# First transfers of memory and weights together, keys in another order, and mLSTM values side by side, in a decoder block on one core

## The chip, the cores and the metric

The kernel runs on one core of one Trainium2 chip. The metric is the device time of one execution in microseconds (us), as a median of runs. Five engines work beside one another: TensorE (PE in the rows, its weight loads PEld), VectorE (DVE), ScalarE (ACT), GpSimd (POOL) and SyncE (SP), which here only issues transfers; 16 DMA engines carry them out.

## The reference

One layer of a decoder block over 256 tokens of width 1024, all in float32. The input is normalized (RMSNorm) and multiplied with a wide matrix that gives queries, keys, values and gates of three mixers:

- NSA: 16 query heads in 4 groups. Each query attends over 15 compressed keys (a small network over 32 tokens each), over selected blocks and over a window; with 256 tokens both of the latter are plain causal attention with their own keys and values. Three softmaxes are gated and summed.
- mLSTM: 4 heads of width 128. In the form used here the 256 x 256 scores of a head, weighted with exponentials of the gates, multiply the values and a column of ones (the normalizer); then comes a norm over the head and a gate.
- Memory attention: 4 heads over 256 memory tokens that have a norm of their own; keys and values are `rmsnorm(mem, g) @ w_kv`.

The three results are projected, gated, summed and projected again, normalized and added to the input. A SwiGLU network of width 2816 with its own norms follows.

## The kernel before

Every float32 product of matrices is made of three products of a shorter format: an operand is split into a high part (ScalarE copies it, `hi`) and a low part (VectorE subtracts, `lo`), and TensorE adds hi x hi, hi x lo and lo x hi in PSUM (`split`, L644, and `mm3`, L666). Weights come in 162 units of 128 x 1024 (`fetch`, L652; 512 KB each), into four buffers `raw`, and are split into `whi` and `wlo`.

The program is first recorded, and then a planner (`schedule`, L353) sets the order of every engine's instructions from costs of its own; `issue` emits them in that order. So all of them carry line 597, and a small change of the program can move instructions anywhere. `FIRST` (L278) is the time at which the planner takes the first matmul to start, `HEAD` (L29) the number of pieces in which each of the first four weight units is split.

At the start TensorE runs ten dummy matmuls (`warm_up(10)`, L732). The memory keys come first (`mem_k`, L784 to L812): SP fetches a weight unit, `m0` (eight columns of gains and the first of eight 256-column blocks of the transposed memory), and the other blocks (`memt`) in two parts. `mem_in(k)` (L767) scales a block with its gain: ScalarE writes `mh`, VectorE `ml`. Each block enters twelve matmuls of 256 columns. Memory values (`mem_v`) and the input's rows (`xn`, `xt`) follow, then the first projections of the input (`hh`, `hl` its parts).

NSA keys lie in `kh` and `kl` (L962), 528 columns per group: 256 of the selected branch with the two halves of the tokens exchanged, 16 compressed, 256 of the window. For the second half of the queries (`nsa_half` with `tb` 1, L1173), each head makes two PSUM tiles `sc`: one of 272 columns (selected and compressed) and one of 256 (window). The causal mask is added by a product of the mask with a bf16 identity (`identb`): three times, on 128, 16 and 128 columns, in each of 16 head-blocks.

mLSTM (`ml_head`, L1091): the weighted scores are split into `sh` and `sl`. With the values and the ones, 130 columns each as high and low part (`vml`), nine matmuls of 130 columns fill `pn`, which has one PSUM buffer (tag `v`, shared with the outputs of NSA and memory attention). VectorE copies numerator and normalizer out, ScalarE squares the numerator from `pn`.

Of the kernel before, what the change touches and what calls it, by code (L numbers as in the profile page):

```python
# [12 lines left out]
F32 = mybir.dt.float32  # L13
# [6 lines left out]
P = 128  # L20
# [6 lines left out]
KF = FF // P  # L27
N_UNITS = 162
HEAD = (2, 2, 1, 1)  # L29
FILL = (5, 7, 1, 1, 1, 1, 1, 1)  # L30
# [137 lines left out]
class Plan:  # L168
# [108 lines left out]
    AHEAD, SWITCH = 1500.0, 1300.0  # L277
    FIRST, DRAIN, PLACE = 5000.0, 4000.0, 200.0  # L278
    ORDER = ("PE", "ACT", "POOL", "DVE", "SP")
# [320 lines left out]
@with_exitstack  # L600
def block_kernel(ctx, tc, order, xN, xT, memN, memT, cst, vec, row, wg, w1, w2, W, out):
    plan = Plan(tc)
# [149 lines left out]

    memt = bigt("G", 3, [P, KD, S], F32, "memt")
    mh = bigt("G", 3, [P, KD, S], F32R, "mh")
# [9 lines left out]

    m0 = work.tile([P, KD + S], F32, tag="sq", bufs=3, name="m0")

    def mem_in(k):  # L767
        gain = m0[:, k:k + 1]
        src = memt[:, k, :] if k else m0[:, KD:]
        ACT.activation(mh[:, k, :], src, AF.Copy, scale=gain)  # L770
        DVE.scalar_tensor_tensor(ml[:, k, :], src, gain, mh[:, k, :].bitcast(F32),
                                 op0=ALU.mult, op1=ALU.subtract)

    def keep_k(i, ps):
# [6 lines left out]
    w2t = one.tile([P, 192], F32, name="w2t")  # L781

    fetch(("mem_k", 0))
    dma(out=m0, in_=memT[:, 0:KD + S])  # L784
    mem_dma = lambda a, b: dma(out=memt[:, a:b, :], in_=memT[:, KD + a * S:KD + b * S].rearrange(
        "p (k s) -> p k s", k=b - a))
    mem_dma(1, 4)
    fetch(("mem_k", 1))
    mem_dma(4, 8)
    warm_up(10)  # L790
    warm = one.tile([P, 1], F32, name="warm")
    ACT.activation(warm, ones[:, 0:1], AF.Copy)
    kps = [ps_d([P, 2, S]) for _ in range(2)]
    for u in range(4):
        if ("mem_k", u) not in ready:
            fetch(("mem_k", u))
        raw = ready.pop(("mem_k", u))
        w = [wpool.tile([P, 1024], F32R, tag=t, bufs=4, name=t) for t in ("whi", "wlo")]
        pieces = HEAD[u]
        for h in range(2):  # L800
            if h < pieces:
                c = slice(1024 // pieces * h, 1024 // pieces * (h + 1))
                split(w[0][:, c], w[1][:, c], raw[:, c])
            mem_in(2 * u + h)
        for k in (2 * u, 2 * u + 1):
            b = lambda j: slice(512 * (k % 2) + P * j, 512 * (k % 2) + P * j + P)
            for i, (x, y) in enumerate(((w[0], mh), (w[1], mh), (w[0], ml))):
# [153 lines left out]

    kk_ = bigt("KK", 1, [P, 2, NG, 528], F32R, "kk")  # L962
    kh, kl = kk_[:, 0], kk_[:, 1]
# [97 lines left out]
    for br in range(2):  # L1061
# [3 lines left out]
        for e in range(2):  # L1065
            r, o = slice(64 * e, 64 * e + 64), slice(64 - 64 * e, 128 - 64 * e)
            for tb in range(2):
                src = kf[r, :, tb * P:(tb + 1) * P]
                c = (P - P * tb, 272 + P * tb)[br]
# [3 lines left out]
            c = slice(272 * br, 272 * br + 256)  # L1073
            for x in (kh, kl):
# [8 lines left out]
    ssq = one.tile([P, 2, 4], F32, name="ssq")  # L1083
    vml = bigt("G", 3, [P, 2, 2, 4, P + 2], F32R, "vml")

    def ml_values():
        split(vml[:, 0, :, :, P:], vml[:, 1, :, :, P:], ones[:, 0:16].rearrange("p (a h d) -> p a h d", a=2, h=4))
        for tb, ps in enumerate(tmaj(X, "v_ml", last=2)):
            split(vml[:, 0, tb, :, 0:P], vml[:, 1, tb, :, 0:P], ps.rearrange("p (h d) -> p h d", h=4))

    def ml_head(h):  # L1091
# [81 lines left out]
    def nsa_half(g, tb, qs, yT):  # L1173
# [4 lines left out]
        for pr in range(2):  # L1178
# [4 lines left out]
            for j in range(2):  # L1183
                q = qs[:, 2 * pr + j, t]
                if tb == 0:
# [3 lines left out]
                    PE.matmul(s[:, 0:272], identb, M0, start=False, stop=True)  # L1189
                    sc = (s[:, P:144], s[:, 0:P], s[:, 144:272])  # L1190
# [24 lines left out]
            for kb in range(nkb):  # L1215
                pt = ps_t([P, 2, 2, P], "ptn")
                for b in range(2):
                    for j in range(2):
                        n = kb if b or not tb else 1 - kb
                        PE.transpose(pt[:, b, j, :], pv4[:, j, b, n * P:(n + 1) * P], ident)  # L1220
# [192 lines left out]
def _layout(inputs):  # L1413
# [4 lines left out]
    xT = ft(a["x"][0].T)  # L1418
    memT = np.concatenate([a["g_mem"][0].reshape(KD, P).T, ft(a["mem"][0].T).reshape(P, KD * S)], axis=1)
    w_in = a["w_in"][0]  # L1420
# [69 lines left out]
    cst[:, K_BM:K_BM + 4] = (i[:, None] // 32) == np.arange(4)[None, :]  # L1490
    arrs = {"xN": a["x"][0], "xT": xT, "memN": a["mem"][0], "memT": memT, "cst": cst, "vec": vec, "row": row, "wg": wg, "w1": w1, "w2": w2}
    return {k: np.ascontiguousarray(v) for k, v in arrs.items()}, units
# [31 lines left out]
```

## Time and profile before

| what | value |
|---|---|
| median of 3 runs (lowest, highest) | 549.82 us (549.79, 551.13) |
| the profiled execution | 550.37 us, span 548.6 us, mean granted clock 0.998 |
| TensorE busy | 539.8 us (98%), 3194 matmuls |
| VectorE, ScalarE, GpSimd busy | 411.6 us (75%), 343.0 us (63%), 26.5 us (5%) |
| DMA | 97.80 MB, 178 GB/s over the span |

The profile is one execution on the chip. The span runs from its first to its last instruction; the rest of the execution's time lies around it. A busy share tells little by itself: matmuls are pipelined and a duration covers the wait inside, so the distance from one start to the next is what a matmul costs the stream.

### The profile page before, as it was taken

What the parts mean: (1) busy time and instruction counts of PE and PEld (TensorE: products, weight loads), DVE (VectorE), ACT (ScalarE), POOL (GpSimd) and SP (SyncE); (2) the same over time, 40 slices, a digit from 0 to 9 for tenths busy, and PEclk for the clock granted to TensorE, in tenths of its full rate; (3) what the DMA queues carried; (4) which work ended last, traced back from release to release, by engine and by line L of the source; (5) the groups of instructions that cost most, each with busy time, mean ns of one, the idle gap of its engine ahead of it and who ended that gap; (6) DMA issues with size and microseconds to landing.
All of it is one profiled execution on the core that took longest, in us unless ns stands there. A gap on an engine that the chain in (4) does not pass through costs nothing.

```text
span 548.6 us, 8855 instructions
## 1 busy us (share of the span) xinstructions
PE 539.8 (98%) x3194; PEld 474.8 (87%) x3194; DVE 411.6 (75%) x799; ACT 343.0 (63%) x676; POOL 26.5 (5%) x43
## 2 busy tenths in 40 slices
PE   9999999999999999999999999999999999999995
PEld 8899998998989889889888888788888888888884
DVE  5795696699989898987878697975777777754543
ACT  7684696576699775965896444754555555553431
POOL 0000000010020111102110000000000000000000
PEclk9999999999999999999999999999999999999999
DMA  8995326526323445345345565654455555555512
GB/s 312 416 396 198 114 107 202 194 79 229 116 79 116 147 176 178 115 154 193 112 157 177 206 217 191 226 173 148 159 192 193 191 189 184 192 185 182 189 70 76
DMA packets 28699, 97.80 MB, mean 178 GB/s; under 512 B 3312, under 2 KB 5488, under 8 KB 28400
## 3 DMA queue, kind: packets, MB, share of 16 engines
q1 hardware_dynamic: 28656, 97.24, 49.7%
q8 instruction: 25, 0.41, 0.3%
q14 instruction: 18, 0.15, 0.1%
HBM read 95.13 MB, written 1.05 MB: 175 GB/s over the span
## 4 chain that ended last, share of the span: by engine, by line
PE 91%; ACT 3%; DMA 2%; DVE 1%; issue 1%; POOL 1%; DVEq 0%; SPq 0%; ACTq 0%
PE pd L597 48%; PE pss L597 30%; PE sc L597 3%; PE pvn L597 2%; DMA raw<-in_W 2%; PE ph L597 2%; PE ptn L597 2%; ACT whi L597 1%; PE pn L597 1%; PE psm L597 1%; PE pgf L597 1%; PE pvm L597 1%; POOL ce L597 1%; PE ptx L597 0%; ACT L597 0%
## 5 line engine op out<-in xcount | busy, mean ns | idle before, releaser
L597 DVE TENSOR_TENSOR wlo<-raw,whi 128x1024 fp32r<-128x1024 f32 (+1 forms) x160 | 194.6, 1222 | 85.7 <-ACT whi L597 84.0
L597 ACT ACTIVATE whi<-raw 128x1024 fp32r<-128x1024 f32 (+1 forms) x160 | 167.3, 1049 | 131.8 <-PE pd L597 65.7
L597 PE MATMUL pd<-hh,wlo 128*128 128x256 f32 x208 | 59.6, 286 | 0.0
L597 PE MATMUL pd<-hl,whi 128*128 128x256 f32 x208 | 59.5, 286 | 0.0
L597 PE MATMUL pd<-hh,whi 128*128 128x256 f32 x208 | 59.3, 285 | 0.0
L597 PE MATMUL pd<-wlo,hh 128*128 128x512 f32 x144 | 58.4, 406 | 0.0
L597 PE MATMUL pd<-whi,hh 128*128 128x512 f32 x144 | 58.2, 404 | 0.0
L597 PE MATMUL pd<-whi,hl 128*128 128x512 f32 x144 | 57.0, 401 | 0.0
L597 PE MATMUL pss<-xc,whi 128*128 128x512 f32 x168 | 43.2, 392 | 0.0
L597 PE MATMUL pss<-whi,u 128*128 128x512 f32 x132 | 42.4, 392 | 0.0
L597 PEld LDWEIGHTS pd<-hh,whi 128*128 128x128 f32 x208 | 39.7, 191 | 0.4 <-DVE on L597 0.2
L597 PEld LDWEIGHTS pd<-hl,whi 128*128 128x128 f32 x208 | 39.8, 191 | 0.1
L597 PEld LDWEIGHTS pd<-hh,wlo 128*128 128x128 f32 x208 | 39.7, 191 | 0.1
L597 PEld LDWEIGHTS pss<-xc,whi 128*128 128x128 f32 x168 | 30.7, 189 | 5.4
L597 PE MATMUL pd<-xc,whi 128*128 128x512 f32 x120 | 31.9, 394 | 0.0
L597 PEld LDWEIGHTS pd<-wlo,hh 128*128 128x128 f32 x144 | 27.2, 189 | 4.4
L597 PEld LDWEIGHTS pd<-whi,hl 128*128 128x128 f32 x144 | 27.2, 189 | 4.3
L597 PEld LDWEIGHTS pd<-whi,hh 128*128 128x128 f32 x144 | 27.2, 189 | 4.2
L597 PEld LDWEIGHTS pss<-whi,u 128*128 128x128 f32 x132 | 24.8, 188 | 5.5
L597 ACT ACTIVATE pp<-sc,mx 128x128 f32<-128x128 f32 (+1 forms) x64 | 26.8, 431 | 1.0 <-DVE mx L597 0.8
L597 DVE TENSOR_REDUCE mx<-sc 128x1 f32<-128x16 f32 (+2 forms) x96 | 22.8, 288 | 6.1 <-PE sc L597 5.9
L597 PE MATMUL pss<-wlo,u 128*128 128x512 f32 x66 | 25.9, 392 | 0.0
(334 smaller groups left out, 1129.9 us busy)
## 6 DMA issues: line engine op xcount, KB each, us to landing
raw<-in_W SPq DMA_DIRECT2D x162, 512.0 KB, 3.2
w<-in_w SPq DMA_DIRECT2D x2, 1024.0 KB, 7.6
xn<-in_xN SPq DMA_DIRECT2D x2, 512.0 KB, 7.3
xt<-in_xT SPq DMA_DIRECT2D x2, 512.0 KB, 8.7
mn<-in_memN SPq DMA_DIRECT2D x2, 512.0 KB, 8.2
kk<-kk SPq DMA_DIRECT2D x8, 128.0 KB, 3.3
x<-in_xN SPq DMA_DIRECT2D x2, 512.0 KB, 3.7
memt<-in_memT SPq DMA_DIRECT2D x1, 512.0 KB, 7.6
```

Of the source, the lines that this page charges most:

```text
L597: op.ins_ = getattr(op.real, op.method)(*map(arg, op.a), **{k: arg(x) for k, x in op.kw.items()})
```

## The change

One input array, `head`, holds gains, first memory block, first weight unit and the other seven blocks side by side, 3080 columns; it comes in four parts, cut so that the first brings the gains, the first block and half of the first weights. The tile takes the place that the keys `kk` have later. The first block's high part is made on VectorE. The third weight unit is split in two pieces in place of one, there are eight dummy matmuls, and the product hi x lo of the inputs comes ahead of that of the weights.

The window keys come first in `kh` and `kl` and the selected ones last, with 16 compressed keys beside either; these are written twice. One mask product covers the 16 and the 128 columns next to them.

`vml` holds per token half and head 258 columns: high values, ones, low values. The second half of the tokens takes high and low values in one matmul of 258 columns; the low values' share is added after, by a ScalarE copy and a VectorE sum. Ones have no low part any more. The squares read the finished numerator.

```diff
-N_UNITS = 162
-HEAD = (2, 2, 1, 1)
+N_UNITS = 161
+HEAD = (2, 2, 2, 1)
...
-    FIRST, DRAIN, PLACE = 5000.0, 4000.0, 200.0
+    FIRST, DRAIN, PLACE = 4300.0, 4000.0, 200.0
...
-    memt = bigt("G", 3, [P, KD, S], F32, "memt")
+    mt = bigt("KK", 1, [P, 3080], F32, "memt")
+    part = lambda a, b: dma(out=mt[:, a:b], in_=head[:, a:b])
...
-        gain = m0[:, k:k + 1]
-        src = memt[:, k, :] if k else m0[:, KD:]
-        ACT.activation(mh[:, k, :], src, AF.Copy, scale=gain)
+        gain = mt[:, k:k + 1]
+        src = mt[:, 8:264] if k == 0 else mt[:, 1032 + k * S:1288 + k * S]
+        if k == 0:
+            DVE.tensor_scalar(mh[:, k, :], src, gain, None, op0=ALU.mult)
+        else:
+            ACT.activation(mh[:, k, :], src, AF.Copy, scale=gain)
...
-    fetch(("mem_k", 0))
-    dma(out=m0, in_=memT[:, 0:KD + S])
-    mem_dma(1, 4)
+    part(0, 776)
+    part(776, 1544)
     fetch(("mem_k", 1))
-    mem_dma(4, 8)
-    warm_up(10)
+    part(1544, 2056)
+    fetch(("mem_k", 2))
+    part(2056, 3080)
+    warm_up(8)
...
-        raw = ready.pop(("mem_k", u))
+        raw = ready.pop(("mem_k", u)) if u else mt[:, 264:1288]
...
-            for i, (x, y) in enumerate(((w[0], mh), (w[1], mh), (w[0], ml))):
+            for i, (x, y) in enumerate(((w[0], mh), (w[0], ml), (w[1], mh))):
...
-    M0, MC1, MT, MD = msk[:, 0:272], msk[:, 272:288], msk[:, 288:416], msk[:, 0:P]
+    M0, MD1, MT, MD = msk[:, 0:272], msk[:, 144:288], msk[:, 288:416], msk[:, 0:P]
...
-    split(kh[:, :, 256:272], kl[:, :, 256:272], pk)
+    twice = [x.rearrange("p g (a c) -> p g a c", a=2)[:, :, :, 256:272] for x in (kh, kl)]
+    split(*twice, pk.unsqueeze(2).to_broadcast([P, NG, 2, 16]))
...
-    vml = bigt("G", 3, [P, 2, 2, 4, P + 2], F32R, "vml")
+    vml = bigt("G", 3, [P, 2, 4, 2 * P + 2], F32R, "vml")
...
-        pn = ps_v([P, 2, P + 2], "pn")
-        for tb, pieces in ((0, ((0, 0),)), (1, ((0, P), (1, S)))):
-            for i, (sb, c0) in enumerate(pieces):
-                mm3(pn[:, tb, :], sh[:, c0:c0 + P], sl[:, c0:c0 + P], vml[:, 0, sb, h, :], vml[:, 1, sb, h, :],
-                    i == 0, i == len(pieces) - 1)
-        DVE.tensor_copy(num[:, :, h, :], pn[:, :, 0:P])
-        DVE.tensor_copy(den[:, :, h:h + 1], pn[:, :, P:P + 1])
+        pn = ps_v([P, 388], "pn")
+        PE.matmul(pn[:, 0:130], sh[:, 0:P], vml[:, 0, h, 0:130], start=True, stop=False, skip_group_check=True)
+        PE.matmul(pn[:, 0:P], sh[:, 0:P], vml[:, 0, h, 130:], start=False, stop=False, skip_group_check=True)
+        PE.matmul(pn[:, 0:130], sl[:, 0:P], vml[:, 0, h, 0:130], start=False, stop=False, skip_group_check=True)
+        for sb, c0 in ((0, P), (1, S)):
+            PE.matmul(pn[:, 130:388], sh[:, c0:c0 + P], vml[:, sb, h, :], start=False, stop=False,
+                      skip_group_check=True)
+            PE.matmul(pn[:, 130:260], sl[:, c0:c0 + P], vml[:, sb, h, 0:130], start=False, stop=sb == 1,
+                      skip_group_check=True)
+        DVE.tensor_copy(num[:, 0, h, :], pn[:, 0:P])
+        ACT.activation(num[:, 1, h, :], pn[:, 260:388], AF.Copy)
+        DVE.tensor_add(num[:, 1, h, :], pn[:, 130:258], num[:, 1, h, :])
+        DVE.tensor_copy(den[:, :, h:h + 1], pn[:, 0:260].rearrange("p (a d) -> p a d", a=2)[:, :, P:P + 1])
...
-            ACT.activation(junk, pn[:, tb, 0:P], AF.Square, accum_out=ssq[:, tb, h:h + 1])
+            ACT.activation(junk, num[:, tb, h, :], AF.Square, accum_out=ssq[:, tb, h:h + 1])
...
-                    for x, c, n in ((s, 0, 272), (s2, 272, 256)):
+                    for x, c, n in ((s, 272, 272), (s2, 0, 256)):
...
-                    PE.matmul(s[:, 0:P], identb, MD, start=False, stop=False, skip_group_check=True)
-                    PE.matmul(s[:, 256:272], identb, MC1, start=False, stop=True, skip_group_check=True)
-                    PE.matmul(s2[:, P:256], identb, MD, start=False, stop=True, skip_group_check=True)
+                    PE.matmul(s[:, P:272], identb, MD1, start=False, stop=True, skip_group_check=True)
+                    PE.matmul(s2[:, 0:P], identb, MD, start=False, stop=True, skip_group_check=True)
```

Three places of the new order. First the transfers that SP issues at the start (`m_74` is the tile `m0`; `raw` a weight unit), before:

```order
L597 DMA m_74<-in_memT 128x264
L597 DMA raw<-in_W 128x1024
L597 DMA memt<-in_memT 128x768
L597 DMA raw<-in_W 128x1024 x2
L597 DMA memt<-in_memT 128x1024
L597 DMA raw<-in_W 128x1024 x2
L597 DMA xn<-in_xN 128x1024 x2
```

and of the change:

```order
L597 DMA memt<-in_head 128x776
L597 DMA memt<-in_head 128x768
L597 DMA memt<-in_head 128x512
L597 DMA raw<-in_W 128x1024
L597 DMA memt<-in_head 128x1024
L597 DMA raw<-in_W 128x1024 x3
L597 DMA xn<-in_xN 128x1024 x2
```

The same bytes are issued ahead of `xn`, but the first transfer is larger and no weight unit stands second; behind `xn` the order is the same up to some 26 us. The orders of TensorE, VectorE and ScalarE are also the same from the end of the memory keys to the first projections of the input.

Then TensorE in the first head-block of the second query half (`sc` scores, `identb` the identity of the mask products), before:

```order
L597 MATMUL sc<-kk,qs 128x272 x2
L597 MATMUL sc<-kk,qs 128x256 x2
L597 LDWEIGHTS identb
L597 MATMUL sc<-msk,identb 128x128
L597 LDWEIGHTS identb
L597 MATMUL sc<-msk,identb 128x16
L597 LDWEIGHTS identb
L597 MATMUL sc<-msk,identb 128x128
```

and of the change:

```order
L597 MATMUL sc<-kk,qs 128x272 x2
L597 MATMUL pvn<-ce_1518,vcs 128x256
L597 MATMUL pvn<-ce_1497,vcs 128x256
L597 MATMUL pvn<-ce_1518,vcs 128x256
L597 MATMUL sc<-kk,qs 128x256 x2
L597 LDWEIGHTS identb
L597 MATMUL sc<-msk,identb 128x144
L597 LDWEIGHTS identb
L597 MATMUL sc<-msk,identb 128x128
```

Two mask products stand in place of three, and three products of the compressed values (`pvn`) have moved between the keys' products. In the whole program the 16 triples and pairs of mask products that held a 16-column one (five triples, eleven pairs) are five pairs and eleven single ones.

Last VectorE behind the products of the second mLSTM head (`pn` the products, `on` the numerator, `wlo` the low part of a weight unit, `mx` maxima of scores), before:

```order
L597 COPY den<-pn 128x2
L597 COPY on<-pn 128x2x128
L597 TENSOR_REDUCE mx<-sc 128x1 x3
L597 TENSOR_TENSOR sl<-dw,sh 128x384
L597 TENSOR_TENSOR wlo<-raw,whi 128x1024 x2
L597 COPY den<-pn 128x2
L597 COPY on<-pn 128x2x128
```

and of the change:

```order
L597 TENSOR_TENSOR sl<-dw,sh 128x384
L597 COPY on<-pn 128x128
L597 COPY den<-pn 128x2
L597 TENSOR_TENSOR wlo<-raw,whi 128x1024
L597 TENSOR_TENSOR on<-pn,on 128x128
L597 TENSOR_REDUCE mx<-sc 128x1 x4
L597 TENSOR_TENSOR sl<-dw,sh 128x384
```

The copy of both halves is a copy of one half; the sum of the other stands behind a subtraction of weights. On TensorE, between the transposition `ptc` of the second NSA half and the first product with GpSimd's result (`pvn<-ce`), there are 29 instructions in place of 19.

## Rows read from the trace of the kernel before

**Rows 1.** The chain that ended last, shares of the span by engine.

```profile
PE 91%; ACT 3%; DMA 2%; DVE 1%; issue 1%; POOL 1%; DVEq 0%; SPq 0%; ACTq 0%
```

**Rows 2.** TensorE's waits: who, for whom, total us, times, longest.

```profile
PE warm L597 <- POOL mhalf L597: 1.0, 1, 1.0
...
PE pvn L597 <- POOL ce L597: 0.4, 1, 0.4
```

**Rows 3.** Timeline, first 8 us: start us, duration us, engine, output<-inputs, count, idle before.

```profile
0.74 0.38 SPq L597 DMA_DIRECT2D m<-in_memT  x1
...
0.99 4.63 PE L597 MATMUL warm<-ones 128*128 128x128 f32 x20 [0.99 <-POOL mhalf L597]
...
5.15 1.15 ACT L597 ACTIVATE whi<-raw 128x512 fp32r<-128x512 f32 x2 [0.69 <-DMA raw<-in_W]
...
5.83 1.17 PE L597 MATMUL pd<-mh,whi 128*128 128x256 f32 x4 [0.21 <-ACT whi L597]
...
6.84 0.63 PE L597 MATMUL pd<-mh,wlo 128*128 128x256 f32 x4
...
7.30 0.64 PE L597 MATMUL pd<-ml,whi 128*128 128x256 f32 x4
```

**Rows 4.** Busy us by engine (count) in a stretch; granted clock, DMA share, GB/s.

```profile
5.83:17.70 11.87, 11.87 (x96) 11.87 (x97) 9.20 (x15) 9.93 (x17) 0.55 (x1) 1.00 1.02 409
```

**Rows 5.** Timeline, 18 to 33 us.

```profile
18.32 1.06 ACT L597 ACTIVATE whi<-raw 128x1024 fp32r<-128x1024 f32 x1 [1.52 <-DMA raw<-in_W]
...
31.44 1.23 DVE L597 TENSOR_TENSOR wlo<-raw,whi 128x1024 fp32r<-128x1024 f32 x1 [0.64 <-ACT whi L597]
...
32.93 0.28 PE L597 MATMUL pss<-hh,wlo 128*128 128x256 f32 x1
```

**Rows 6.** Transfers of the first 25 us: count, size, median us from issue to landing.

```profile
m<-in_memT SPq DMA_DIRECT2D x1, 132.0 KB, 3.2
```

**Rows 7.** Transfers of weight units (tile `raw`, 512 KB each), first 30 us.

```profile
DMA to landing us min/median/max: 4.0/7.6/8.9
```

**Rows 8.** Timeline of TensorE, two head-blocks of the second query half.

```profile
121.94 0.65 PE L597 MATMUL sc<-kk,qs 128*128 128x272 f32 x4
122.43 0.31 PE L597 MATMUL sc<-msk,identb 128*128 128x128 bf16 x3
122.55 0.50 PE L597 MATMUL sc<-kk,qs 128*128 128x272 f32 x2
122.89 0.24 PE L597 MATMUL sc<-msk,identb 128*128 128x128 bf16 x2
...
142.81 0.23 PE L597 MATMUL sc<-msk,identb 128*128 128x128 bf16 x1
142.84 0.73 PE L597 MATMUL sc<-kk,qs 128*128 128x272 f32 x4
143.41 0.31 PE L597 MATMUL sc<-msk,identb 128*128 128x128 bf16 x3
```

**Rows 9.** Timeline of TensorE, a head's nine products (176.62 to 177.57), then projections.

```profile
176.62 0.34 PE L597 MATMUL pn<-vml,sh 128*128 128x130 f32 x2
...
177.57 0.46 PE L597 MATMUL sc<-kk,qs 128*128 128x272 f32 x2
...
178.23 0.39 PE L597 MATMUL pd<-whi,hh 128*128 128x512 f32 x1
178.46 0.40 PE L597 MATMUL pd<-wlo,hh 128*128 128x512 f32 x1
```

**Rows 10.** VectorE's groups by form, 165 to 185 us: count, busy us, mean ns, idle before.

```profile
L597 DVE TENSOR_TENSOR wlo<-raw,whi 128x1024 fp32r<-128x1024 f32 x5 | 6.9, 1388 | 0.0
...
L597 DVE COPY on<-pn 128x256 f32<-128x256 f32 x4 | 1.7, 418 | 0.0
```

**Rows 11.** The chain that ended last, 140 to 185 us: start us, us, what.

```profile
162.42 2.04 POOL ce L597
```

**Rows 12.** Busy us by engine in a stretch, columns as in Rows 4.

```profile
170.00:180.00 10.00, 10.00 (x72) 8.98 (x72) 9.84 (x27) 8.85 (x30) 0.00 (x0) 1.00 0.14 47
```

More of the change, by code (lines that the diff above doesn't have):

```diff
@@ L600, in block_kernel @@
 @with_exitstack
-def block_kernel(ctx, tc, order, xN, xT, memN, memT, cst, vec, row, wg, w1, w2, W, out):
+def block_kernel(ctx, tc, order, xN, xT, memN, head, cst, vec, row, wg, w1, w2, W, out):
     plan = Plan(tc)
@@ L763, in block_kernel @@
     rmb = one.tile([P, S], F32, tag="bcs", name="rmb")
-    m0 = work.tile([P, KD + S], F32, tag="sq", bufs=3, name="m0")
     def mem_in(k):
-        gain = m0[:, k:k + 1]
-        src = memt[:, k, :] if k else m0[:, KD:]
-        ACT.activation(mh[:, k, :], src, AF.Copy, scale=gain)
+        gain = mt[:, k:k + 1]
[4 more added lines that the diff above has]
+            ACT.activation(mh[:, k, :], src, AF.Copy, scale=gain)
         DVE.scalar_tensor_tensor(ml[:, k, :], src, gain, mh[:, k, :].bitcast(F32),
@@ L781, in block_kernel @@
     w2t = one.tile([P, 192], F32, name="w2t")
-    fetch(("mem_k", 0))
-    dma(out=m0, in_=memT[:, 0:KD + S])
-    mem_dma = lambda a, b: dma(out=memt[:, a:b, :], in_=memT[:, KD + a * S:KD + b * S].rearrange(
-        "p (k s) -> p k s", k=b - a))
-    mem_dma(1, 4)
+    part(0, 776)
+    part(776, 1544)
     fetch(("mem_k", 1))
-    mem_dma(4, 8)
-    warm_up(10)
+    part(1544, 2056)
+    fetch(("mem_k", 2))
+    part(2056, 3080)
+    warm_up(8)
     warm = one.tile([P, 1], F32, name="warm")
@@ L794, in block_kernel @@
     for u in range(4):
-        if ("mem_k", u) not in ready:
+        if u and ("mem_k", u) not in ready:
             fetch(("mem_k", u))
-        raw = ready.pop(("mem_k", u))
+        raw = ready.pop(("mem_k", u)) if u else mt[:, 264:1288]
         w = [wpool.tile([P, 1024], F32R, tag=t, bufs=4, name=t) for t in ("whi", "wlo")]
@@ L959, in block_kernel @@
     ACT.activation(em, nmf, AF.Exp)
-    kk_ = bigt("KK", 1, [P, 2, NG, 528], F32R, "kk")
+    kk_ = bigt("KK", 1, [P, 2, NG, 544], F32R, "kk")
     kh, kl = kk_[:, 0], kk_[:, 1]
@@ L1068, in block_kernel @@
                 src = kf[r, :, tb * P:(tb + 1) * P]
-                c = (P - P * tb, 272 + P * tb)[br]
+                c = (272 + P * tb, P - P * tb)[br]
                 c = slice(c, c + P)
@@ L1072, in block_kernel @@
                 DVE.tensor_sub(kl[r, e::2, c], src, kh[r, e::2, c].bitcast(F32))
-            c = slice(272 * br, 272 * br + 256)
+            c = slice(272 * (1 - br), 272 * (1 - br) + 256)
             for x in (kh, kl):
@@ L1083, in block_kernel @@
     ssq = one.tile([P, 2, 4], F32, name="ssq")
-    vml = bigt("G", 3, [P, 2, 2, 4, P + 2], F32R, "vml")
+    vml = bigt("G", 3, [P, 2, 4, 2 * P + 2], F32R, "vml")
     def ml_values():
-        split(vml[:, 0, :, :, P:], vml[:, 1, :, :, P:], ones[:, 0:16].rearrange("p (a h d) -> p a h d", a=2, h=4))
+        ACT.activation(vml[:, :, :, P:P + 2], ones[:, 0:16].rearrange("p (a h d) -> p a h d", a=2, h=4), AF.Copy)
         for tb, ps in enumerate(tmaj(X, "v_ml", last=2)):
-            split(vml[:, 0, tb, :, 0:P], vml[:, 1, tb, :, 0:P], ps.rearrange("p (h d) -> p h d", h=4))
+            split(vml[:, tb, :, 0:P], vml[:, tb, :, P + 2:], ps.rearrange("p (h d) -> p h d", h=4))
     def ml_head(h):
@@ L1189, in nsa_half @@
                     PE.matmul(s[:, 0:272], identb, M0, start=False, stop=True)
-                    sc = (s[:, P:144], s[:, 0:P], s[:, 144:272])
+                    sc = (s[:, P:144], s[:, 144:272], s[:, 0:P])
                 else:
                     s, s2 = ps_s([P, 512], "sc"), ps_s([P, 512], "sc")
-                    for x, c, n in ((s, 0, 272), (s2, 272, 256)):
+                    for x, c, n in ((s, 272, 272), (s2, 0, 256)):
                         PE.matmul(x[:, 0:n], q, kh[:, g, c:c + n], start=True, stop=False, skip_group_check=True)
                         PE.matmul(x[:, 0:n], q, kl[:, g, c:c + n], start=False, stop=False, skip_group_check=True)
-                    PE.matmul(s[:, 0:P], identb, MD, start=False, stop=False, skip_group_check=True)
-                    PE.matmul(s[:, 256:272], identb, MC1, start=False, stop=True, skip_group_check=True)
-                    PE.matmul(s2[:, P:256], identb, MD, start=False, stop=True, skip_group_check=True)
+                    PE.matmul(s[:, P:272], identb, MD1, start=False, stop=True, skip_group_check=True)
+                    PE.matmul(s2[:, 0:P], identb, MD, start=False, stop=True, skip_group_check=True)
                     sc = (s[:, 256:272], s[:, 0:256], s2[:, 0:256])
@@ L1218, in nsa_half @@
                     for j in range(2):
-                        n = kb if b or not tb else 1 - kb
+                        n = 1 - kb if b and tb else kb
                         PE.transpose(pt[:, b, j, :], pv4[:, j, b, n * P:(n + 1) * P], ident)
@@ L1418, in _layout @@
     xT = ft(a["x"][0].T)
-    memT = np.concatenate([a["g_mem"][0].reshape(KD, P).T, ft(a["mem"][0].T).reshape(P, KD * S)], axis=1)
     w_in = a["w_in"][0]
@@ L1490, in _layout @@
     cst[:, K_BM:K_BM + 4] = (i[:, None] // 32) == np.arange(4)[None, :]
-    arrs = {"xN": a["x"][0], "xT": xT, "memN": a["mem"][0], "memT": memT, "cst": cst, "vec": vec, "row": row, "wg": wg, "w1": w1, "w2": w2}
+    memT = ft(a["mem"][0].T).reshape(P, KD * S)
+    head = np.concatenate([a["g_mem"][0].reshape(KD, P).T, memT[:, 0:S], units["mem_k", 0], memT[:, S:]], axis=1)
+    arrs = {"xN": a["x"][0], "xT": xT, "memN": a["mem"][0], "head": head, "cst": cst, "vec": vec, "row": row, "wg": wg, "w1": w1, "w2": w2}
     return {k: np.ascontiguousarray(v) for k, v in arrs.items()}, units
```

## Prediction

> **What bounds the kernel now.** I read the chain that ended last first: TensorE has 91% of it [rows 1]. Then the list of what TensorE waited for: five entries, the first 1.0 us before the very first matmul, the others 0.4 us or less [rows 2]. So the matmul stream runs through, and a change shortens the kernel by what it takes out of that stream, by how much earlier the stream starts, or by the small waits it removes or adds. VectorE and ScalarE matter where they feed it just in time, and that is the third thing to read, stretch by stretch.
>
> The start is the first stretch. The first real matmuls begin at 5.83 us, 0.68 us after ScalarE starts to split the first weights at 5.15; that split waited for their transfer [rows 3]. The dummy matmuls (20 instructions for ten calls) take 4.63 us from 0.99. [...]
>
> From 5.83 to 17.70 the 16 DMA engines are fully busy (share 1.02, 409 GB/s) [rows 4]. At 18.32 ScalarE has idled 1.52 us for a transfer of weights; from there splits, scaled inputs and weights follow one another closely, and at the end of that sequence VectorE writes the low part of a weight unit from 31.44 to 32.67, which TensorE takes at 32.93 [rows 5]. The spare time there is 0.26 us.
>
> **The start, term by term.** Now 132 KB (gains and first memory block) must land, and then 512 KB (first weights). After the change one transfer of 776 columns x 128 rows x 4 bytes = 388 KB brings the gains, the first block and the first half of the weights. The 132 KB took 3.2 us from issue to landing, the quickest 512 KB of weights 4.0 [rows 6, 7]. Between them 388 KB are 3.2 + 0.8 x 256/380 = 3.74 us; issued at 0.74 it lands at 4.48. The bounds are the landings of the two: 3.94 and 4.74. With the 0.68 us of the split, matmuls start at 5.16 (4.62 to 5.42) in place of 5.83. VectorE scales the first block beside ScalarE's split, so it adds nothing there. Eight dummy calls in place of ten are 16 instructions, 4.63 x 16/20 = 3.70 us, over at 4.69: they bind only at the earliest bound. So the lead is 0.67 us, with 0.41 to 1.14 as its bounds.
>
> How much of it lasts? [...] And after that the landings: the bytes queued before the weights that ScalarE awaited at 18.32 are the same, and the engines are saturated on the way, so those weights land when they land now unless the queue fills better in the first 6 us. Then TensorE can be only 0.26 us ahead at 32.9, and waits off the rest. I take 0.3 us (the two nearest figures, 0.33 and 0.26), and keep 0 and 1.14 as ends. The order of the three products matters little: the low part of the inputs comes from one VectorE instruction ahead of the low weights now, and takes the middle place.
>
> **One mask product in place of two.** With the new key order the causal mask of the first window and the compressed mask lie side by side, so 16 + 128 columns become one product of 144 in each of 16 head-blocks (4 groups, 4 heads, the second half of the queries). The price of such a small bf16 product in this stream is read by difference. Four key products take 122.43 - 121.94 = 0.49 us, so two take 0.245. Three masks and two key products take 122.89 - 122.43 = 0.46, so the three masks 0.215. One mask and four key products take 143.41 - 142.81 = 0.60, so one mask alone 0.11 [rows 8]. Two more masks cost 0.105, one of them 0.05. Sixteen removed are 0.8, less some 0.1 for 16 x 16 = 256 further columns: 0.7 us. The bounds are 0 (where the next weight load binds anyway) and 16 x 0.11 = 1.8.
>
> **mLSTM values side by side.** Per head nine products of 130 columns become seven: five of 128 or 130, two of 258. The nine take 177.57 - 176.62 = 0.95 us, 0.106 each [rows 9]; products of 256 columns go at 0.46/4 = 0.115 [rows 3]. Seven are 5 x 0.106 + 2 x 0.115 = 0.76, so a head saves 0.19 and four save 0.75 us. The bounds are 0, since the columns hardly fall (1170 to 1164), and 2 x 0.106 x 4 = 0.85. [...]
>
> What it adds is off TensorE. Per head VectorE does two instructions of 128 columns for one of 256 (0.42 us) [rows 10] and ScalarE one copy more; in return ScalarE's squares read SBUF and no longer the bank. One split of the ones falls away on VectorE. The cost stands at nothing because TensorE has other work meanwhile; if that cover is gone it is the last rival's price.
>
> **A wait that the new order covers.** The longest of the 0.4 us waits is for GpSimd, whose second masking product takes 2.04 us [rows 11]. In the new order 29 instructions stand in place of 19 between the transposition that starts this and the matmul that needs it. Ten at 0.115 are 1.1 us, more than the wait: 0.4 gained. The other positions move a few matmuls either way; I set these at nothing, within plus or minus 0.5.
>
> **The sum.** 0.3 + 0.7 + 0.75 + 0.4 = 2.15 us, rounded to 2.1. The profiled execution took 550.37 us with a span of 548.6; it becomes 548.3 with a span of 546.5. It lies 0.55 above the median of the runs, 549.82, so the median becomes 547.7.
>
> **Rivals.**
> *The landings hold the stream.* The weights land as now or a little later, since the first transfer is three times as large, and the lead is waited off by 33 us; the small products give half of what I reckon, because their neighbours then wait for weight loads. For it: DMA share 1.02 and ScalarE's wait at 18.32. Against it: the first transfer keeps the engines busy sooner. Then 0 + 0.35 + 0.4 + 0.1 = 0.85 us: 549.0.
>
> *The queue fills sooner.* The large first piece fills the time in which the engines now have only 132 KB; landings move ahead with the start, the pace too. Then 1.14 + 0.9 + 0.85 + 0.4 = 3.3 us: 546.5. Against it speaks that all of it must happen together.
>
> *The bank of the mLSTM products is held longer: slower.* These products have one PSUM buffer. Now two short VectorE copies and ScalarE's squares free it. In the new order, after the second head, a weight subtraction stands on VectorE between two of its readers: 1.39 us more [rows 10]. VectorE is busy 9.84 of the 10 us there [rows 12], with the score maxima and the next head's low scores queued behind, so it cannot catch up. It decides from the point where the last reader ends later than what TensorE has to do between two heads: in the new order a dozen matmuls, eight of them of 512 columns at 178.46 - 178.23 = 0.23 us each [rows 9], so some 2.2 us with the narrow ones. Copy and sum at the 0.42 us of today's copy at most, and 1.39 between them, are 2.2 us: it just fits behind that head. If every head pays the 1.39 us, less some 0.4 of spare work in each, it is 4 x 1.0 = 4.0 us: 549.8 - 2.1 + 4.0 = 551.7. For it: the new position. Against it: it stands so behind one head only.
>
> **How the numbers follow.** What a measurement of this kernel can tell from no change is about 0.3%, 1.65 us, so the line lies at 548.2. My forecast has 0.50, of which 0.42 falls beyond the line and 0.08 short of it, as it lies only 0.5 us past it. The held stream has 0.27, the sooner queue 0.13, the held bank 0.10. So faster 0.42 + 0.13 = 0.55, same 0.08 + 0.27 = 0.35, slower 0.10. The range runs from 546.4, the sooner queue, to 549.9, past the held stream's 549.0 by the unknown moves of the order; it leaves out the held bank. The likeliest case alone is 547.1 to 548.4.
>
> **What would show it.** The first real matmul starts near 5.2 us. The low part taken at 32.93 is taken 0.3 us earlier, with new idle of TensorE in front of it if the lead was larger. The group of three masks is gone; two stand in it, and head-blocks are shorter by 0.05 us. The seven products of a head take 0.76 us. GpSimd is gone from TensorE's waits. [...]

## The result and the profile after

The changed kernel takes 547.89 us in the median of five runs (546.63 to 548.30); the kernel before, run on the same chip between them, 550.73 (549.79 to 551.13). The ratio is 0.9949 with an interval of 0.9932 to 0.9967: faster, by 1.8 to 3.7 us. The profiled execution took 546.63 us with a span of 544.8, where before took 550.37 and 548.6.

The chain that ended last, by engine, where [rows 1] had 91% for TensorE:

```profile
PE 88%; DVE 5%; DMA 2%; ACT 2%; issue 1%; POOL 0%; SPq 0%; DVEq 0%; ACTq 0%
```

TensorE still has nearly all of it, but more of the start now runs through transfers and splits. TensorE's waits, with the columns of [rows 2], complete:

```profile
PE warm L597 <- POOL mhalf L597: 1.0, 1, 1.0
PE pd L597 <- ACT whi L597: 0.8, 1, 0.8
PE pvn L597 <- POOL ce L597: 0.4, 1, 0.4
```

Two things are to be seen. The wait for GpSimd's masking product, which I had counted as covered, is still there. And there is a wait of 0.8 us for ScalarE's split of the second weight unit. Three waits of before are not in the list: `ptc` for `pTl` on VectorE, 0.4 us, one of 0.2 us for the first split, and one of 0.2 us for ScalarE's `xc`, which is there again in other executions.

The timeline of the first 10 us, which answers to [rows 3]:

```profile
0.99 3.46 PE L597 MATMUL warm<-ones 128*128 128x128 f32 x16 [0.99 <-POOL mhalf L597]
...
3.91 0.64 ACT L597 ACTIVATE whi<-memt 128x512 fp32r<-128x512 f32 x1 [1.27 <-DMA memt<-in_head]
...
4.60 0.74 PE L597 MATMUL pd<-mh,whi 128*128 128x256 f32 x4
...
5.18 0.62 PE L597 MATMUL pd<-ml,whi 128*128 128x256 f32 x4
...
7.75 1.15 ACT L597 ACTIVATE whi<-raw 128x512 fp32r<-128x512 f32 x2 [1.03 <-DMA raw<-in_W]
...
8.43 0.74 PE L597 MATMUL pd<-mh,whi 128*128 128x256 f32 x4 [0.83 <-ACT whi L597]
```

The first transfer has landed when ScalarE starts at 3.91 us, the first real matmul starts at 4.60, 1.23 us earlier than before, and the first four take 0.58 from start to start, where before's took 1.01. Then TensorE has run out of weights: the second unit lands at 7.7, and 0.83 us of the lead are waited off.

Where the time went is read best from the same matmuls in both profiles. The table takes the starts of the same instructions from the timelines: the first matmul of the query projections, at 35.57 before; the stretch from the first score product (107.30) to the merge behind attention (309.37); from the merge's last transposition to the feed-forward part; and that part's two halves, the first from 380.08 to 481.07. The names in the first column are those of the experiments below.

| kernel | first real matmul | query projections | attention | up to feed-forward | first half | second half |
|---|---|---|---|---|---|---|
| before | 5.83 | 35.57 | 202.07 | 43.56 | 100.99 | 60.51 |
| before_again | 5.54 | 35.90 | 202.08 | 44.14 | 100.99 | 60.51 |
| changed | 4.60 | 35.13 | 199.98 | 43.60 | 100.26 | 59.86 |
| again | 4.68 | 35.54 | 200.00 | 44.21 | 100.25 | 59.86 |
| late_start | 5.87 | 34.99 | 200.00 | 44.55 | 100.26 | 59.86 |

Attention gives 2.1 us, and the two halves of the feed-forward part, whose instructions the change does not touch, 0.73 and 0.65. These repeat to 0.02 us. What varies from one execution to the next are the start, by up to a microsecond, and the stretch ahead of the feed-forward part, where TensorE waits for ScalarE's `xc`, 1.2 us in masks_two and in the changed kernel's profile not at all.

### The profile page after: what moved, and what is told of

Its sections match the earlier page's. It is cut to its first block, busy times and chain, and to the rows that moved or that the text cites. A ratio compares the mean times of both kernels' runs of the same rounds, so it can differ in the third digit from the quotient of the medians.

```text
span 544.8 us, 8802 instructions
## 1 busy us (share of the span) xinstructions
PE 535.7 (98%) x3166; PEld 469.8 (86%) x3166; DVE 412.1 (76%) x804; ACT 342.7 (63%) x680; POOL 29.4 (5%) x43
## 3 DMA queue, kind: packets, MB, share of 16 engines
HBM read 95.13 MB, written 1.05 MB: 177 GB/s over the span
## 4 chain that ended last, share of the span: by engine, by line
PE 88%; DVE 5%; DMA 2%; ACT 2%; issue 1%; POOL 0%; SPq 0%; DVEq 0%; ACTq 0%
PE pd L597 46%; PE pss L597 29%; PE sc L597 3%; PE pvn L597 2%; DMA raw<-in_W 2%; PE ph L597 2%; PE ptn L597 2%; DVE wlo L597 1%; DVE cy L597 1%; ACT whi L597 1%; PE ptx L597 1%; DVE xt L597 1%; PE pn L597 1%; PE psm L597 1%; PE pgf L597 1%
```

## The experiments

In all of them the order of the instructions is that of the kernel named, except where the edit says otherwise. Each was timed in five rounds with the kernel before on the same chip, whose median lay between 550.6 and 551.2 us.

**again.** No edit.

> The changed kernel once more, nothing edited. Theory (the surplus in the feed-forward part belongs to the kernel): the 256-column matmuls between 380 and 480 us again follow one another at about 113.5 ns, and the lead over the kernel before again grows there by some 1.3 us. Rival (it belongs to the one execution): they go at about 118.8 ns, as in the profile of the kernel before, and the time in that execution is 1 to 1.5 us longer than 546.6. Both expect a median near 547.9, and TensorE's wait for GpSimd's masking product (0.4 us) again.

Median 547.28 us, ratio 0.9935 (0.9918 to 0.9951). The pace of 113.5 ns came again, as in all variants of this order that leave the places in memory alone: it belongs to the kernel. The rival falls. The wait for GpSimd was there again.

**masks_two.** One mask product becomes two, when it is issued:

```
+ if op.method == "matmul" and op.a[0].tile.name == "sc" and op.a[0].shape[1] == 144:
+     calls = [((o[:, 0:128], w, x[:, 0:128]), dict(op.kw, stop=False)), ((o[:, 128:144], w, x[:, 128:144]), op.kw)]
```

> The changed kernel with each of its 16 mask products of 144 columns issued as one of 128 and one of 16 columns; the order of everything else is unchanged. Theory (a small product costs what it takes in the stream): a head-block's masks go back from 0.18 to 0.20 us where two masks stand and from 0.12 to 0.18 where one stands, 16 products together +0.7 us, so about 548.6 against 547.9. Rival (the neighbours' weight loads bind anyway): head-blocks keep their time and the kernel stays at 547.9. Second rival (each product at the price of a lone one, 0.11): +1.8 us, 549.7.

Median 548.03 us. The attention stretch as a window (columns as in [rows 4]), of the changed kernel and of this one:

```profile
106.87:306.85 199.98, 199.59 (x1236) 175.32 (x1234) 172.13 (x431) 147.74 (x364) 22.67 (x20) 1.00 0.43 150
```

```profile
107.24:307.96 200.72, 200.32 (x1252) 176.05 (x1251) 172.12 (x431) 147.92 (x364) 22.62 (x20) 1.00 0.44 149
```

Sixteen matmuls more, 0.74 us longer, and the same idle of TensorE (0.4 us) in both: the sixteen products cost 0.05 each, as reckoned. They don't cost alike, though. Measured from the first mask to the second projection behind it, less that projection's usual time, 11 groups of (128, 16) take 0.177 us and of (144) 0.122, a difference of 0.055; in the five groups where a further mask follows it is 0.018.

**values_two.** Each wide product in an mLSTM head becomes two:

```
+ if op.method == "matmul" and op.a[0].tile.name == "pn" and op.a[0].shape[1] == 258:
+     calls = [((o[:, 0:130], w, x[:, 0:130]), op.kw), ((o[:, 130:258], w, x[:, 130:258]), op.kw)]
```

> The changed kernel with each of the eight products of 258 columns in the mLSTM heads issued as one of 130 and one of 128 columns; the order of everything else is unchanged. Theory (a product has a price of its own beside its columns): nine products of a head take about 0.95 us again in place of 0.75, so four heads +0.8 us, 548.7 against 547.9. Rival (only columns cost): +0.02 us, a head's products stay at 0.75 us.

Median 548.54 us. The head's products on TensorE, first of the changed kernel, then of this one:

```profile
174.90 0.33 PE L597 MATMUL pn<-vml,sh 128*128 128x130 f32 x2
...
175.18 0.33 PE L597 MATMUL pn<-vml,sh 128*128 128x258 f32 x1
175.35 0.23 PE L597 MATMUL pn<-vml,sl 128*128 128x130 f32 x1
175.42 0.33 PE L597 MATMUL pn<-vml,sh 128*128 128x258 f32 x1
...
175.65 0.47 PE L597 MATMUL sc<-kk,qs 128*128 128x272 f32 x2
```

```profile
175.92 0.33 PE L602 MATMUL pn<-vml,sh 128*128 128x130 f32 x2
...
176.88 0.46 PE L602 MATMUL sc<-kk,qs 128*128 128x272 f32 x2
```

From the first product to what follows it is 0.75 us with seven and 0.96 with nine. Over attention the undone change costs 200.86 - 200.00 = 0.86 us. So a product of 130 columns has a price of 0.1 us, and only columns cost is refuted. A wide product takes 0.17 itself and the narrow one behind it 0.06 to 0.07: the trace has the load of the next weights start at 175.23, 0.05 us into the wide one.

**late_start.** Four more dummy calls ahead of the first real matmul:

```
+ for _ in range(5 if warm and self.warm == 8 else 1):
```

> The changed kernel with 12 dummy calls in place of eight ahead of the first real matmul, which then starts 0.8 to 1.7 us later than at 4.6 us. Theory (landings hold the lead of the start to about 0.45 us by 33 us): TensorE waits less at 28 to 35 us, the stream behind 35 us is at most 0.4 us later, and the median 0 to 0.4 us above 547.9. Rival (every tenth at the start counts to the end): 0.8 to 1.7 us above, 548.7 to 549.6.

Median 547.22 us, 0.06 under again. TensorE in the first 10 us:

```profile
0.99 5.13 PE L600 MATMUL warm<-ones 128*128 128x128 f32 x24 [0.99 <-POOL mhalf L600]
...
5.87 0.72 PE L600 MATMUL pd<-mh,whi 128*128 128x256 f32 x4
...
8.78 0.64 PE L600 MATMUL pd<-mh,whi 128*128 128x256 f32 x4
```

The first real matmul comes 1.2 us later, and nothing is lost: the wait for the second unit is gone in place of it, and at 35 us this execution is even 0.14 us ahead of the changed kernel's. The rival, that every tenth at the start counts, is refuted. What sets the stream in the other profiles is a landing. ScalarE's split of the second value unit started at 19.57 in the changed kernel's profile, at 19.98 in again and 20.36 in values_two, and the matmuls of the last low part at 32.05, 32.46 and 32.84: 12.48 us behind it each time (12.47 in masks_two and ce_turn), and each time a matmul is held at 28.4 to 29.6. In late_start they are 12.55 us apart, 19.42 and 31.97, and no matmul is held on the way: stream and landing come out nearly even there. In again the wait stands out, TensorE first and ScalarE below:

```profile
29.17 0.38 PE L597 MATMUL pss<-hh,wlo 128*128 128x256 f32 x1 [0.35 <-DVE wlo L597]
```

```profile
19.98 1.06 ACT L597 ACTIVATE whi<-raw 128x1024 fp32r<-128x1024 f32 x1 [1.88 <-DVE wlo L597]
```

ScalarE idled 1.88 us ahead of this split. The label names a VectorE instruction there and the transfer of the weights in the changed kernel's and late_start's profiles; but the transfer lands 0.10 us ahead of the split in all of them, in again at 19.88.

**ce_turn.** On VectorE the short subtraction `cl` changes places with the low part of the weights ahead of it:

```
+ j = [i for i in range(len(n)) if name(i) == "cl"][1]
+ order[n[j - 1]], order[n[j]] = order[n[j]], order[n[j - 1]]
```

> The changed kernel with two neighbours on VectorE exchanged ahead of TensorE's wait for GpSimd: the short subtraction that feeds GpSimd's second masking product goes before the low part of the weights. Theory (a GpSimd product on SBUF and a VectorE instruction with two SBUF sources exclude one another; who starts first goes first): the first masking product starts beside the short subtraction, which reads PSUM, and takes 1.04 us in place of 1.66; the low part, now behind it, takes longer than 1.22 us or starts only when the product has ended; TensorE waits for that low part, about 1 us, at 161 to 163 us, and the kernel is 0.5 to 1 us slower. Rival (the product is slowed by something else, as ScalarE or a transfer): it still takes 1.66 us, and the low part 1.22.

Median 548.30 us, attention 200.49 us in place of 199.98. GpSimd and VectorE around the place, first of the changed kernel:

```profile
160.67 1.66 POOL L597 TENSOR_TENSOR ce<-ch,cs 128x512 fp32r<-128x512 f32 x1 [18.64 <-ACT ch L597]
162.30 2.02 POOL L597 TENSOR_TENSOR ce<-cl,cs 128x512 fp32r<-128x512 f32 x1
```

```profile
160.21 1.22 DVE L597 TENSOR_TENSOR wlo<-raw,whi 128x1024 fp32r<-128x1024 f32 x1
161.34 0.29 DVE L597 TENSOR_TENSOR cl<-ptc,ch 128x128 f32<-128x128 f32 x1
161.54 0.69 DVE L597 COPY on<-pd 128x512 f32<-128x512 f32 x1
162.14 3.26 DVE L597 TENSOR_TENSOR wlo<-raw,whi 128x1024 fp32r<-128x1024 f32 x2
```

And of ce_turn:

```profile
160.91 1.05 POOL L602 TENSOR_TENSOR ce<-ch,cs 128x512 fp32r<-128x512 f32 x1 [18.64 <-ACT ch L602]
161.92 2.03 POOL L602 TENSOR_TENSOR ce<-cl,cs 128x512 fp32r<-128x512 f32 x1
```

```profile
160.87 0.29 DVE L602 TENSOR_TENSOR cl<-ptc,ch 128x128 f32<-128x128 f32 x1 [0.33 <-ACT ch L602]
161.07 1.97 DVE L602 TENSOR_TENSOR wlo<-raw,whi 128x1024 fp32r<-128x1024 f32 x1
```

With the low part behind it, the first product takes 1.05 in place of 1.66 us, and the low part 1.97 in place of 1.22: each pays when it comes second. In the changed kernel's trace a product that starts beside a low part (seven of 16) lasts until that has ended and some 0.9 us more; the others take 1.04, but for one of 1.22 at 117.85, beside another VectorE instruction. Among those of 1.04 are one beside `cl` alone, at 243.54, and one beside the maxima `mx`, at 228.01, both of which read PSUM. That much of the theory the traces show; whether the two SBUF sources are the reason was not tried. The wait that I expected, about 1 us for the low part at 161 to 163, did not come. TensorE's wait for GpSimd is gone, but it then waits 0.7 us for ScalarE's `dw`, because ScalarE waited 2.88 us, in place of 1.71, for VectorE's copies, which stand behind the longer low part.

**Places in memory.** The change gives the key tile's buffer the first place among the large SBUF buffers, since the first transfer lands in it, and makes it 512 bytes larger. All addresses move with that. The feed-forward inputs lie in this buffer. The next seven runs ask whether this is the 1.4 us.

**before_again.** No edit.

> The kernel before once more, nothing edited, for its second profile. Theory (the pace in the feed-forward part belongs to the kernel): 256-column matmuls between 380 and 480 us again follow at about 118.8 ns, 512-column ones behind 480 us at 228 to 230.5, and the part from 380.1 us to the last matmul again takes 161.5 us (160.1 in the five profiles of the changed kernel and its variants). Rival (a matter of the execution): somewhere else, down to 160.1. At the start both expect the first real matmul near 5.8 us, and the stream at the low part (32.61) within 0.4 us of that, since five profiles of the changed start spread from 31.97 to 32.84 there.

Median 551.15 us; 118.8 ns and 161.5 us again, the matmuls of the last low part at 32.93, in place of 32.61.

**before_moved** and **after_moved.** The buffers are named once, in the order wanted, ahead of the program (in the second all of them, with `KK_0` last):

```
+ for tag in "KK_0".split():
+     big.tile([P, 1024], F32, tag=tag, bufs=1, name="place")
```

> The kernel before with the same instructions in the same order, but the buffer that holds the key tile and later the feed-forward inputs is given the first place of the large SBUF buffers, as the changed kernel does, in place of the last; the weight buffers stay where they are. Theory (the place of the feed-forward inputs in SBUF sets the pace of the matmuls that read them): 256-column matmuls go at 113.5 ns in place of 118.8 and the feed-forward part takes 160.1 us in place of 161.5, so the median is 1.3 to 1.4 us under the kernel before, 549.4 to 549.8 where that has 551. Rival (the weight buffers' place, or the other tiles): 118.8 ns, no difference in time.

> The changed kernel with the same instructions in the same order, but the large SBUF buffers are given their places in the order in which the kernel before has them, the key tile and feed-forward inputs last; the weight buffers stay where the changed kernel has them. Theory (the inputs' place sets the pace): 118.8 ns in place of 113.5 in the feed-forward part, 161.5 us in place of 160.1, and the median 1.3 to 1.4 us above the changed kernel's 547.3 to 547.9, about 548.9. Rival (the weight buffers' place): 113.5 ns and 547.3 to 547.9.

Medians 552.08 us (ratio 1.0020, 1.0011 to 1.0028) and 547.65. The second flipped as the theory had it, 118.8 ns and 100.97 us in the first half; the first did not, and was even slower (101.56). So the inputs' place alone is not it. The median of after_moved does not show the 0.6 us that its profile is longer in the feed-forward part (548.9 was expected). Both profiles can be read by the distance between inputs and weights.

**before_weights** and **before_placed.** Now the weight buffers, `whi_0 raw_0 wlo_0 ...`, are named first in the changed kernel's order too, with the key tile's buffer 448 bytes larger; in the second that buffer also stands first.

> The kernel before, same instructions in the same order, with the weight buffers (raw, high, low) at the addresses and in the sequence that they have in the changed kernel, 448 bytes further; the feed-forward inputs stay in the last place. Theory (the places of the two operands of a matmul set its pace together): the second half of the feed-forward part, which reads these weights and other inputs, goes at 227 ns for 512 columns in place of 230, 54.4 us in place of 55.1; the first half stays at 118.8 and 230 ns, 101.0 us. Together 0.7 us less than the kernel before, about 550.4. Rival (what TensorE does earlier, or how the other engines interleave, sets it): 55.1 us and no difference in time.

> The kernel before, same instructions in the same order, with both: the weight buffers at the changed kernel's addresses, and the buffer of the key tile and the feed-forward inputs in first place. Theory (the two places together): 113.5 and 231.8 ns in the first half, 100.3 us, and 227 ns in the second, 54.4 us: the whole part 160.1 us in place of 161.5 and the median 1.3 to 1.4 us under the kernel before, about 549.7. Rival (the edits themselves bring the pace): 161.5 us, no difference.

Medians 551.21 and 550.48 us. before_placed has the changed kernel's first half, 100.25 us, but not its second, 60.56; its median is no different from before's (ratio 0.9997, 0.9988 to 1.0006), its profile was late at the start (6.40). before_weights has an even shorter first half, 99.68, but the second is 60.74, and attention takes 203.35 us in place of before's 202.07, with the same instructions in the same order.

**after_shift.** 64 bytes of padding behind the inputs:

```
+ big.tile([P, 4368], F32, tag="KK_0", bufs=1, name="place")
```

> The changed kernel with 64 bytes of padding behind the buffer of the feed-forward inputs: those inputs stay at byte 29824, everything behind them, the weights with it, moves by 64 bytes. In the runs so far the 256-column matmuls of the first half of the feed-forward part went at 113.5 to 115 ns where weights and inputs lay 64 bytes apart modulo 128, and at 118 to 119 where they lay 0 apart. Theory (that distance sets the pace of these matmuls): 118 to 119 ns in place of 113.5, the first half 100.9 to 101.6 us in place of 100.26, the second half unchanged at 59.86; the median 0.7 to 1.3 us above 547.5. Rival (it is the absolute place, or the sequence of the buffers): 113.5 ns and 100.26 us.

**before_full.** The large buffers in the changed kernel's sequence with a gap of 64 bytes, so that all distances are as there modulo 128.

> The kernel before, same instructions in the same order, with all the large buffers placed nearly as in the changed kernel, so that the same distances modulo 128 hold: feed-forward inputs against weights 64, two of the six tiles of the second half's inputs against weights 64, the other four 0. Theory (these distances set the pace): first half 100.25 us in place of 100.99, second half 59.86 in place of 60.51, together 1.4 us less; the median about 549.7 where the kernel before has 551.1. Rival (the second half's pace comes from something else than the places): first half 100.25, second 60.5, the median 550.4.

after_shift: median 548.13 us, ratio 0.9957 (0.9945 to 0.9969). The first half as a window, of the changed kernel and of this one:

```profile
377.64:477.91 100.27, 100.27 (x584) 87.48 (x583) 75.64 (x126) 58.54 (x107) 0.00 (x0) 1.00 0.53 189
```

```profile
377.44:479.04 101.60, 101.60 (x584) 88.79 (x583) 75.66 (x126) 58.59 (x107) 0.00 (x0) 1.00 0.56 187
```

The same 584 matmuls, TensorE never idle, the same work on VectorE and ScalarE, and 1.33 us more for 64 bytes. The second half stayed at 59.86. The medians don't separate the two kernels, since their intervals overlap; the reading rests on the profiles. Here the inputs stayed and the weights moved, with everything else behind the inputs; in after_moved the weights stayed and the inputs moved. Either brought the slower pace, so it is the distance and not one operand's place. The others fit it (addresses by the built programs):

| kernel | inputs at byte | weights from | distance mod 128 | 256 columns, ns | 512, ns | first half | second half |
|---|---|---|---|---|---|---|---|
| before | 128256 | 145152 | 0 | 118.8 | 229.9 | 100.99 | 60.51 |
| before_moved | 29824 | 145152 | 0 | 118.1 | 232.1 | 101.56 | 60.52 |
| after_moved | 128192 | 145600 | 0 | 118.8 | 230.0 | 100.97 | 59.74 |
| after_shift | 29824 | 145664 | 0 | 118.0 | 232.1 | 101.59 | 59.86 |
| changed | 29824 | 145600 | 64 | 113.5 | 231.8 | 100.26 | 59.86 |
| before_placed | 29824 | 145600 | 64 | 113.5 | 231.8 | 100.25 | 60.56 |
| before_weights | 128256 | 145600 | 64 | 115.2 | 228.3 | 99.68 | 60.74 |
| before_full | 29824 | 145728 | 64 | 115.2 | 228.3 | 99.72 | 60.67 |

(The ns are the mean from start to start, of matmuls followed by one of the same width, between 400 and 460 us, without the longest tenth.) before_full's theory fell in the second half: 60.67 us, and the median, 551.52, is no better than before's.

But modulo 128 is too coarse. Taken modulo 256, weights less inputs, the distance is 0 in before and after_moved, 64 in changed and before_placed, 128 in before_moved and after_shift, 192 in before_weights and before_full. The two layouts of each pair agree to 0.1 ns in both columns of ns and to 0.04 us in the first half, though in three of the pairs the addresses differ. So before_full never had the changed kernel's distances.

The second half can be read in the same way. Here the weights are what streams through, 512 columns at a time, and the inputs are six tiles at places of their own. From start to start a matmul took 227.0 ns in the mean where weights less tile is 0 modulo 256, 229.1 at 64, 232.5 at 128 and 233.2 at 192 (a tile's mean lies within 1.6 ns of these in all eight layouts). The kernel before has three tiles at 0 and three at 128; the changed kernel has four at 0 and two at 64. The stretch as a window, before and changed:

```profile
481.07:541.60 60.53, 60.53 (x265) 49.46 (x263) 29.03 (x34) 24.87 (x31) 0.00 (x0) 1.00 0.41 148
```

```profile
477.91:537.79 59.88, 59.88 (x265) 49.38 (x263) 29.06 (x34) 24.85 (x31) 0.00 (x0) 1.00 0.42 150
```

The four means, times the matmuls at each distance, give the second half of every layout in the table within 0.07 us: 60.49 before, 59.89 changed, 60.74 in before_weights (three tiles at 64, three at 192), 60.68 in before_full (two at 0, two at 128, two at 192). after_moved, the changed kernel's instructions at other places (five tiles at 0, one at 64), is 0.12 us shorter than the changed kernel, where the means give 0.10. So by this reading the 0.65 us come from the places too; no layout of the kernel before had the changed kernel's distances there. It was read off the runs afterwards, and no run was made to test it.

## Why the prediction was right, and where not

The median, 547.89 us, is 0.2 from the forecast of 547.7. Two errors cancel in that. The sum was 2.1 us, and the gain was 1.8 to 3.7 us in the first comparison, 2.7 to 4.5 in again; the spans of the two profiles differ by 3.7. And I subtracted from 549.82, the median of three runs, where later medians of the kernel before are 550.6 to 551.2: the base was about 1 us too low. I saw the profile lie 0.55 above the median, and should have kept that as an uncertainty of the base.

*The start, 0.3 us.* The size came out, but single executions vary by more: over the profiles with the old start the query projections begin at 35.65 us (mean of six, 35.50 to 35.93), with the new one at 35.32 (mean of eight, 34.76 to 35.93), 0.33 earlier. The working holds in part. The lead of the first matmul was 1.23 us, more than my upper bound of 1.14: the first transfer took 3.15 us (landed at 3.89) where I had 3.74. In this execution the matmuls stand 0.11 to 0.13 us apart from the second, at 4.82, to the wait at 8.43, where before's do only from 6.84 on; in that of masks_two, which starts at 4.62, they do only from 6.50 on. That the lead would be cut at the landings was right: late_start gives it all up and loses nothing. So the 0.33 us are not what is left of the lead, as I had it, and that they came out at my 0.3 is luck. The 0.33 that the prediction names beside 0.26, a share of the lead, no run shows; in its place late_start shows a first matmul 1.27 us later (5.87 in place of 4.60) and the query projections 0.14 earlier (34.99 in place of 35.13). I had taken the weights awaited at 18.32 to land when they did; they landed at 16.73 in place of 18.21, and the unit behind them, which then held the stream, at 19.47 in place of 19.80. And I set the cut by the 0.26 us of spare time at the low part that was taken at 32.93; the waits came earlier, 0.83 us at 8.43 for the second unit, and up to 0.5 at 28.4 to 29.6 ahead of the low part before that one.

*Masks, 0.7 us.* masks_two: 0.72 to 0.74, by the attention stretch. The timeline of TensorE at the second place of [rows 8]:

```profile
142.32 0.23 PE L597 MATMUL sc<-msk,identb 128*128 128x128 bf16 x1
142.36 0.73 PE L597 MATMUL sc<-kk,qs 128*128 128x272 f32 x4
142.93 0.29 PE L597 MATMUL sc<-msk,identb 128*128 128x144 bf16 x2
```

The group of three is gone and two stand in it, as foretold. The 0.05 is an average over 0.055 in eleven groups and 0.018 in five.

*mLSTM values, 0.75 us.* values_two: 0.86 us; a head 0.75 us in place of 0.96. Nine and seven products of equal columns differ by 0.21 us. The 0.106 us for a product of 130 columns [rows 9] held: the nine of values_two take 0.107 each.

*The covered wait, 0.4 us: this step failed.* I counted matmuls between the transposition and the matmul that needs its result, "29 instructions in place of 19", and took GpSimd's time as fixed, 2.04 us for the second product, which already was one beside a low part. GpSimd did start 0.75 us earlier (160.67 in place of 161.42), but in the new order a low part stands beside its first product, which took 1.66 us in place of 1.04, and the second again 2.02. It ended at 164.32, against 164.45 before, and TensorE waited 0.39 us as ever. That another wait of 0.4 us, of `ptc` for `pTl`, went away in the new order was luck, and why it went was not tried: the terms of the order that I had set at nothing, within 0.5, hold it. Attention without masks and values is 2.09 - 0.72 - 0.86 = 0.5 us shorter, and 0.38 of it is idle that is gone (202.07 - 201.30 before, 199.98 - 199.59 after).

*Not in the sum: 1.4 us of the feed-forward part.* I did not ask what a larger and earlier buffer does to the addresses of everything else. For 0.73 of it after_shift shows the cause; the 0.65 follow from the same distances, tile by tile.

The rivals: *the landings hold the stream* was right on the start and wrong on the small products, which gave what was reckoned. *The queue fills sooner* needed the pace to come with the start, which it did in some executions, and the landings to move. The first value unit's did, by 1.5 us between the two first profiles; the second's, the one that counts, hardly did: its split starts at 19.94 us in the mean of the six profiles with the old start and at 19.74 in that of the eight with the new one. *The bank held longer* did not come: no wait of TensorE for VectorE's sum is in the list, and attention got shorter.

## What to carry to other kernels

Before counting a lead at the start as a gain, find the first landing behind it that the stream must wait for: here 1.2 us of lead could be given up at no cost, and the whole new start was worth 0.33 in the mean. When counting what covers a wait on GpSimd, look at what VectorE does beside it in the new order, since a product there takes 1.04 or 1.66 or 2.02 us by who started first. And when a change moves buffers, compare the pace of the matmuls in stretches that it does not touch, before its gain is put down to its edits.

## What the runs showed of the hardware

With TensorE always busy and the granted clock at 1.00, the pace of the feed-forward matmuls went by the distance of the two operands' addresses modulo 256, weights less inputs, in eight layouts:

| distance | 256 columns, first half | 512, first half | 512, second half |
|---|---|---|---|
| 0 | 118.8 ns | 229.9 to 230.0 | 227.0 |
| 64 | 113.5 | 231.8 | 229.1 |
| 128 | 118.0 to 118.1 | 232.1 | 232.5 |
| 192 | 115.2 | 228.3 | 233.2 |

In the first half the inputs stream and the weights stay; in the second it is the other way round. For 64 bytes of padding that is 1.33 us of 101. Other distances were not tried, nor how it comes about, nor whether a placement that takes the best of each stretch would beat the changed kernel.
